# Bonus sums moved behind the prep and tied to gate blocks; keys and betas relaid so that one 128x128 transpose serves a head pair

## The chip, the core and the metric

The kernel runs on one core of a Trainium2 chip, in one launch. The metric is the device time in microseconds (us) of that launch. The engines are named as in the profile: PE is TensorE (PEld its weight load), DVE is VectorE, ACT is ScalarE, POOL is GpSimd, SP is SyncE. ACT, SP and POOL also issue DMAs; an engine's queue of issues stands in line with its instructions.

## What is computed

The reference is one block of a hybrid encoder on a sequence of 512 frames of width 1024: an input projection, an RWKV-7 branch (8 heads of 64) beside a gated linear recurrence, a merge by gates, cross-attention on 256 memory rows, and a gated feed-forward part. The change is all in the RWKV-7 branch. Cut to what matters of it:

```python
kk = k * k_k                       # then made of unit length for each head
k  = k * (1.0 + (a - 1.0) * k_a)   # the keys; the betas are kk * a
S_t = S_{t-1} diag(w_t) + (S_{t-1} a_t) b_t^T + v_t k_t^T
y_t = S_t r_t                      # a_t = -kk, b_t = kk * a
y   = group_norm(y) * lnx_g + lnx_b
bonus = jnp.sum(r * k * r_k, axis=-1, keepdims=True) * v
out = (y + bonus) * g
```

The bonus is a sum over the 64 channels of each head of r·k·r_k, times v. It doesn't enter the recurrence; it is added after the group norm.

## The kernel before

Channels lie on the 128 partitions (two heads of 64, a *pair*), the 512 frames run along the free axis. There are 4 pairs (NPAIR) and 8 chunks of 64 frames (NC). A float32 product is made as three fp32r matmuls of a high and a low part (mm3, L160 to L162), so a projection block of 128 output channels (`in_ps`) takes 24 matmuls of 512 columns, and its weights come by SP's queue as `win_r`, are split on ACT (`win_h`, L114) and on DVE (`win_l`, L115).

The input projection runs 14 RWKV blocks first (IN_RWKV) and then the 24 blocks of IN_REST, of which 16 are gate blocks: projection, sigmoid on ACT (`gs`), and a store to the DRAM buffer dG from ACT's queue. Blocks 22 to 24 (NEARLY = 3) are written ahead of the last pair's prep, the others after. They are the filler that keeps PE at work beside the RWKV steps.

For each pair j come, in this order: prep (L543 on: low-rank products, decay, unit length of kk), prep2 (which multiplies keys and betas by the inverse decay into KBt, L576 to L580, and writes AK), scores (16 products of 128 columns each per half, PE L605, masked by DVE into BZ and AK, L609 and L610; BZ goes out to dM), and bonus. The bonus multiplies r, k and r_k on DVE (`pr`, L586), splits the product into `bo_h` (ACT, L154) and `bo_l` (DVE, L155), sums over each head by two matmuls against a block of ones (`bo`, L156 and L157), multiplies by v (DVE, L589), adds lnx_b (ACT, L590) and stores to dBo[j] in DRAM from ACT's queue (L591).

After the four pairs, the prep's pool (pp) is closed and its memory is used again. `Zt` (the inverse of 32x32 triangles, solved on DVE, L655 to L661) takes over memory of it: its first memset, on DVE, waits until the store of the last pair's `pr` to dBo has landed. `Nm` is read back from dM for the solve. Then 32x32 products (zh, L687, and zo, L695), and the recurrence over 8 chunks: per chunk the products vr, x, y, u and s, and `rows_kb` (L741 to L748), which turns keys and betas of the next chunk from columns into rows by 8 transposes on PE (L746), each of 64 partitions by 128 columns, four into each of two PSUM banks ("kv" and "s"), and two copies on ACT (L747) into KBr. The group norm (L815 on) loads the bonus back from dBo (L821).

The order of the work on each engine is set by a scheduler from the order of the program text, priorities and dependences; each engine then runs its own list in order, so that an instruction that waits holds all that stands behind it on its engine.

Of the kernel before, what the change touches and what calls it, by code (L numbers as in the profile page):

```python
# [9 lines left out]
F32 = mybir.dt.float32  # L10
# [7 lines left out]
P = 128  # L18
# [12 lines left out]
IN_RWKV = [12, 13, 4, 5, 0, 1, 8, 9, 6, 7, 2, 3, 10, 11]  # L31
IN_REST = [22, 23, 24, 25, 26, 27, 28, 29, 30, 31, 32, 33, 34, 35, 36, 37, 14, 15, 16, 17, 18, 19, 20, 21]
NEARLY = 3
IN_ORDER = IN_RWKV + IN_REST


# [17 lines left out]
def hybrid_block_kernel(ctx: ExitStack, tc: tile.TileContext, xT_d, mT_d, pv_d, cst_d, win_d, wk_d, wv_d,  # L54
# [118 lines left out]
    def dense(ps, units, rhs, nkb, nsum=0):  # L173

        for kb in range(nkb):
            wh, wl = units.next()
            rh, rl = rhs(kb)
            ins = mm3(ps, wh, wl, rh, rl, kb == 0, kb == nkb - 1)
            if kb * nsum % nkb < nsum:
                sum_behind(ins)  # L180

    class Split:

# [294 lines left out]
    pa_ctx = ExitStack()  # L478
    pa = pa_ctx.enter_context(tc.tile_pool(name="pa", bufs=1, reuse_waits="tile"))
    BZ = pa.tile([P, NPAIR * NC, P], F32, tag="AR", name="BZ")  # L480
    KBt = big.tile([P, NPAIR, 2 * NC + 1, HD], F32, tag="x16", name="KBt")
    vT = pa.tile([P, NPAIR, T], F32, name="vT")
    AK = pa.tile([P, 2, NPAIR * NC, P], F32, tag="SC", name="AK")
    PC = pa.tile([P, NPAIR, NC], F32, name="PC")
# [22 lines left out]
    for i in range(2):  # L507
        with tc.issue_after(wdma[-1].ins):
            nc.sync.dma_start(lraw[i], lup_d[i])
    uin = Units(win_d, "win")  # L510


    NSUM = {12: 1, 13: 1, 4: 1, 5: 1, 0: 1, 1: 1, 8: 1, 9: 1, 6: 2, 7: 2, 2: 2, 3: 2, 10: 2, 11: 2,
            22: 2, 23: 1, 27: 1, 28: 1, 29: 1, 15: 4, 16: 4, 17: 4, 18: 4, 19: 4, 20: 3, 21: 2}

    def inproj(i):
        ps = mm_ps(f"in_ps{i}")
        dense(ps, uin, lambda kb: (h2[:, 0, kb, :], h2[:, 1, kb, :]), KB, NSUM.get(i, 0))
        return ps

    def evac_shift(ps, blk, out):
# [39 lines left out]
    def prep2(j, pk, pr, at, Pi, Pp):  # L561
        c3 = lambda a: a.rearrange("p (c t) -> p c t", t=HD)
        kk = pp.tile([P, T], F32, tag="kk", name=f"kk{j}")
        S.activation(kk, pk, AF.Copy, scale=par("k_k", j))
        sq = pp.tile([P, T], F32, tag="q", name=f"sq{j}", bufs=2)
        S.activation(sq, kk, AF.Square)
        ps = rw_ps(f"ss{j}")
        sum_exact(ps, bonesr, sq, tp, "xb", f"ss{j}")
        tab.rsqrt(sq, ps, 1.0, eps[:, 2:3])
        V.scalar_tensor_tensor(kk, sq, 1e12, kk, ALU.min, ALU.mult)  # L570
        jc = slice(j * NC, (j + 1) * NC)
        for e in range(2):
            hs = half[e]
            V.scalar_tensor_tensor(AK[hs, e, jc, 0:HD], c3(kk)[hs], -1.0, Pp[hs, :, 0:HD], ALU.mult, ALU.mult)
        V.tensor_tensor(kk, kk, at, ALU.mult)
        V.tensor_tensor(KBt[:, j, 1::2, :], c3(kk), c3(Pi), ALU.mult)  # L576
        S.activation(at, at, AF.Identity, scale=par("k_a", j), bias=oka[:, j:j + 1])
        V.tensor_tensor(pk, pk, at, ALU.mult)
        V.tensor_tensor(KBt[0:HD, j, 2::2, :], c3(pk)[0:HD], c3(Pi)[0:HD], ALU.mult)
        V.tensor_tensor(KBt[HD:P, j, 0:2 * NC:2, :], c3(pk)[HD:P], c3(Pi)[HD:P], ALU.mult)  # L580
        for e in range(2):
            hs = half[e]
            V.tensor_tensor(AK[hs, e, jc, HD:P], c3(pr)[hs], Pp[hs, :, 1:], ALU.mult)

    def bonus(j, pk, pr):
        V.scalar_tensor_tensor(pr, pr, par("r_k", j), pk, ALU.mult, ALU.mult)  # L586
        ps = rw_ps(f"bo{j}")
        sum_exact(ps, bonesr, pr, tp, "xb", f"bo{j}")
        V.tensor_tensor(pr, ps, vT[:, j, :], ALU.mult)  # L589
        S.activation(pr, pr, AF.Identity, bias=par("lnx_b", j))  # L590
        nc.scalar.dma_start(dBo[j], pr)  # L591

    def kb_cols(j, e, c):
        return KBt[half[e], j, 2 * c + 1 - e:2 * c + 3 - e, :].rearrange("p a t -> p (a t)")

    def scores(j):
        for e in range(2):
            hs, oh = half[e], half[1 - e]  # L600
            for cg in range(2):
                ps = rw_ps(f"sc{j}_{e}_{cg}")
                i0 = j * NC + cg * 4
                for i in range(4):
                    PE.matmul(ps[:, i * P:(i + 1) * P], kb_cols(j, e, cg * 4 + i), AK[hs, e, i0 + i, :],  # L605
                              start=True, stop=True)
                p3 = ps.rearrange("p (c t) -> p c t", t=P)
                m3 = scmask.unsqueeze(1).to_broadcast([P, 4, P])
# [12 lines left out]
    for jp in range(2):  # L621
# [10 lines left out]
        for j in js:  # L632
            if j == 3:
                for i in IN_REST[:NEARLY]:
                    gate_block(i - 22)
            at, L, Pp = prep(j)
            prep2(j, pks[j], prs[j], at, L, Pp)
            scores(j)
            bonus(j, pks[j], prs[j])

    pp_ctx.close()
    pq_ctx = ExitStack()
    pq = pq_ctx.enter_context(tc.tile_pool(name="pq", bufs=1, reuse_waits="tile"))
    YB = pq.tile([P, 4, T], F32, name="YB")


    with tc.tile_pool(name="pz", bufs=1, reuse_waits="tile") as pz:
# [91 lines left out]
        return UV  # L739

    def rows_kb(c):  # L741
        KBr = ch.tile([P, 2, NPAIR, HD], F32, tag="KBr", name=f"KBr{c}", bufs=2)
        for e in range(2):
            ps = ch_ps(f"kbr{c}_{e}", ("kv", "s")[e])
            for j in range(NPAIR):
                PE.transpose(ps[:, j * HD:(j + 1) * HD], kb_cols(j, e, c), ident[half[e], half[e]])  # L746
            S.copy(KBr[:, e], j3(ps[:, 0:256]))  # L747
        return KBr  # L748

    def pc_b(c):  # L750
# [2 lines left out]
    def chunk(c, UV, KBr, SP):  # L753
# [22 lines left out]
        if not last:  # L776
            nUV = rows_v(c + 1)
            pss = ch_ps(f"s{c}", "s")
            for j in range(NPAIR):
                for e in range(2):  # L780
                    PE.matmul(pss[half[e], j * HD:(j + 1) * HD], KBr[:, e, j, :], UV[:, e, j, :],
                              start=True, stop=True)
        for j in range(NPAIR):
            for e in range(2):
# [633 lines left out]
```

## Time and profile before

| | |
|---|---|
| time, 3 runs | 913.08, 912.09, 909.4 us; median 912.09 |
| the profiled execution | 909.73 us, its span 908.0 us |
| PE busy | 890.5 us (98% of the span) |
| DVE, ACT, POOL busy | 687.4, 510.4, 129.3 us |
| chain that ended last | PE 28%, DVE 1%, the rest below 1% |

The profile is of one execution. It gives the busy time of each engine, the waits of each engine with what ended them, and every instruction with its start and length. A matmul's length overlaps the next one's, so that PE's price for a matmul is read from one start to the next. An idle time in brackets behind a row is that of the engine just before the instruction, with what ended it.

### The profile page before, as it was taken

The numbers are of one execution on the slowest core, as the hardware profiler recorded it, in microseconds if no ns is written. First come the engines' busy times: TensorE is split into PE (matmuls) and PEld (weight loads), VectorE is DVE, ScalarE is ACT, GpSimd is POOL, SyncE is SP. The second block draws the span as 40 slices with busy tenths as digits, with TensorE's granted clock in tenths as the row PEclk, the third lists the DMA queues.
The fourth block names the chain that finished last, engine by engine and source line by source line (L and its number), as shares of the span: only waits on it lengthen the run. The fifth ranks groups of instructions, "written<-read, shape, count | busy, mean of one in ns | idle before, by whom it ended". The sixth has DMA issues, their size and how long they took to land. (4 is left out here: it accounts for less than half of the span.)

```text
span 908.0 us, 15914 instructions
## 1 busy us (share of the span) xinstructions
PE 890.5 (98%) x6218; PEld 776.1 (85%) x6218; DVE 687.4 (76%) x1096; ACT 510.4 (56%) x779; POOL 129.3 (14%) x159
## 2 busy tenths in 40 slices
PE   7999999999999999999999999999999999999996
PEld 6988877788877777887887778999999999999996
DVE  7884598776957585776565568788998888999674
ACT  6674675542236675234454446765665556767663
POOL 0102222010011212001112211111111111201100
PEclk9999999999999999999999999999999999999999
DMA  8878899667499749858788868898989998998963
GB/s 276 277 263 230 186 237 208 179 165 206 139 205 246 167 106 194 258 180 223 210 243 190 177 152 185 240 273 247 280 249 290 258 316 251 248 277 222 269 197 93
DMA packets 102411, 200.07 MB, mean 220 GB/s; under 512 B 25344, under 2 KB 36736, under 8 KB 102272
## 3 DMA queue, kind: packets, MB, share of 16 engines
q1 hardware_dynamic: 69504, 119.75, 41.0%
q0 software_dynamic: 25504, 67.38, 36.8%
q10 hardware_dynamic: 7328, 11.92, 3.9%
q8 instruction: 49, 0.80, 0.3%
q14 instruction: 26, 0.21, 0.1%
HBM read 187.75 MB, written 77.59 MB: 292 GB/s over the span
## 5 line engine op out<-in xcount | busy, mean ns | idle before, releaser
L126 ACT CAST wfi_h<-wfi_r 128x1024 fp32r<-128x1024 f32 x77 | 81.0, 1052 | 76.8 <-PE fx_ps L161 21.1
L160 PE MATMUL in_ps<-hT,win_h 128*128 128x512 f32 x304 | 121.9, 402 | 0.8 <-DVE pr L525 0.7
L162 PE MATMUL in_ps<-hT,win_l 128*128 128x512 f32 x304 | 120.8, 398 | 0.0
L161 PE MATMUL in_ps<-hT,win_h 128*128 128x512 f32 x304 | 120.6, 398 | 0.0
L127 DVE TENSOR_TENSOR wfi_l<-wfi_r,wfi_h 128x1024 fp32r<-128x1024 f32 x77 | 94.0, 1221 | 23.5 <-ACT wfi_h L126 23.3
L425 POOL DMA_DIRECT2D dS<-in_wfi x66 | 66.5, 1044 | 267.0 <-PE in_ps L160 132.4
L114 ACT CAST win_h<-win_r 128x1024 fp32r<-128x1024 f32 x38 | 39.8, 1048 | 71.9 <-PE in_ps L161 70.9
L115 DVE TENSOR_TENSOR win_l<-win_r,win_h 128x1024 fp32r<-128x1024 f32 x38 | 46.4, 1221 | 32.6 <-ACT win_h L114 32.5
L160 PEld LDWEIGHTS in_ps<-hT,win_h 128*128 128x128 f32 x304 | 57.0, 187 | 15.6 <-DVE pr L525 1.1
L161 PEld LDWEIGHTS in_ps<-hT,win_h 128*128 128x128 f32 x304 | 57.0, 188 | 14.0 <-issue 0.7
L162 PEld LDWEIGHTS in_ps<-hT,win_l 128*128 128x128 f32 x304 | 57.0, 187 | 13.9 <-issue 0.2
L461 POOL DMA_DIRECT2D dOs<-in_wfo x54 | 39.9, 804 | 186.0 <-PE fx_ps L160 50.9
L1245 DVE TENSOR_TENSOR wfo_l<-wfo_r,wfo_h 128x1024 fp32r<-128x1024 f32 (+1 forms) x39 | 47.2, 1210 | 13.6 <-ACT wfo_h L1244 13.5
L1244 ACT CAST wfo_h<-wfo_r 128x1024 fp32r<-128x1024 f32 (+1 forms) x39 | 40.4, 1038 | 28.2 <-PE oyz_ps L161 9.8
L161 PE MATMUL fx_ps<-hr,wfi_h 128*128 128x256 f32 x176 | 49.7, 282 | 0.0
L162 PE MATMUL fx_ps<-hr,wfi_l 128*128 128x256 f32 x176 | 49.7, 282 | 0.0
L160 PE MATMUL ox_ps<-go,wfo_h 128*128 128x256 f32 x176 | 49.6, 282 | 0.1
L160 PE MATMUL fyz_ps<-hq,wfi_h 128*128 128x256 f32 x176 | 49.3, 280 | 0.4 <-ACT p L1173 0.4
L160 PE MATMUL fx_ps<-hq,wfi_h 128*128 128x256 f32 x176 | 49.5, 281 | 0.0
L160 PE MATMUL fx_ps<-hr,wfi_h 128*128 128x256 f32 x176 | 49.4, 281 | 0.0
L162 PE MATMUL ox_ps<-go,wfo_l 128*128 128x256 f32 x176 | 49.3, 280 | 0.0
L161 PE MATMUL ox_ps<-go,wfo_h 128*128 128x256 f32 x176 | 49.3, 280 | 0.0
(418 smaller groups left out, 2727.8 us busy)
## 6 DMA issues: line engine op xcount, KB each, us to landing
dS<-in_wfi POOLq DMA_DIRECT2D x66, 512.0 KB, 8.4
wfi_r<-dS SPq DMA_DIRECT2D x44, 512.0 KB, 6.9
win_r<-in_win SPq DMA_DIRECT2D x38, 512.0 KB, 5.0
wfi_r<-in_wfi SPq DMA_DIRECT2D x33, 512.0 KB, 5.6
dS<-dS POOLq DMA_DIRECT2D x22, 512.0 KB, 5.7
dOs<-in_wfo POOLq DMA_DIRECT2D x12, 512.0 KB, 7.8
wv_r<-in_wv SPq DMA_DIRECT2D x8, 512.0 KB, 4.9
dG<-gs ACTq DMA_DIRECT2D x16, 256.0 KB, 2.6
```

The costliest lines, as they stand in the source:

```text
L114: S.copy(hi[:, o:o + n], raw[:, o:o + n])
L115: V.tensor_tensor(lo[:, o:o + n], raw[:, o:o + n], hi[:, o:o + n].bitcast(F32), ALU.subtract)
L126: S.copy(hi, raw)
L127: V.tensor_tensor(lo, raw, hi.bitcast(F32), ALU.subtract)
L160: first = PE.matmul(ps, lh, rh, start=start, stop=False, **kw)
L161: PE.matmul(ps, lh, rl, start=False, stop=False, **kw)
L162: PE.matmul(ps, ll, rh, start=False, stop=stop, **kw)
L425: return lambda: nc.gpsimd.dma_start(s(out), src, **kw)
L461: yield lambda k=k, w=w, src=src: nc.gpsimd.dma_start(dO[n, m][:, k * P:(k + w) * P], src, **kw)
L1244: S.copy(hi[:, :n], raw[:, :n])
L1245: V.tensor_tensor(lo[:, :n], raw[:, :n], hi[:, :n].bitcast(F32), ALU.subtract)
```

## The change

There are two parts.

*The bonus.* Inside the loop over pairs, only the product is left (`bonus_terms`): `pr` is stored to dBo[j] as it is. After the prep's pool is closed, the four products are loaded again (`bt`, ACT's queue), rounded by ACT into `bhi`, and the rest is taken by DVE into `blo`. Then gate blocks 25 to 29 (up to NMID = 8) follow, and after each from the second on the two sum matmuls of a pair, held by `issue_after` until the first product of the last mm3 of that gate block has issued. The product with v, lnx_b and the store to dBo[j] go with them (`bs`). `bhi` takes the memory that YB has later; `bt` and `bs` share two buffers.

*The layout.* KBt loses its one spare column group. In one partition half the keys stand before the betas, in the other the betas before the keys, so that the columns of one chunk are a full 128x128 square for both heads. `rows_kb` becomes 4 transposes of 128x128 into one bank and one ACT copy of 128x512, and the writes of KBt become four DVE operations on 64 partitions for each pair, where there were one on 128 and two on 64.

```diff
+NMID = 8
@@ dense
+        return ins
@@
-    KBt = big.tile([P, NPAIR, 2 * NC + 1, HD], F32, tag="x16", name="KBt")
+    KBt = big.tile([P, NPAIR, 2 * NC, HD], F32, tag="x16", name="KBt")
@@ inproj
-        dense(ps, uin, lambda kb: (h2[:, 0, kb, :], h2[:, 1, kb, :]), KB, NSUM.get(i, 0))
+        last_in = dense(ps, uin, lambda kb: (h2[:, 0, kb, :], h2[:, 1, kb, :]), KB, NSUM.get(i, 0))
@@ prep2
-        V.tensor_tensor(KBt[:, j, 1::2, :], c3(kk), c3(Pi), ALU.mult)
-        V.tensor_tensor(KBt[0:HD, j, 2::2, :], c3(pk)[0:HD], c3(Pi)[0:HD], ALU.mult)
-        V.tensor_tensor(KBt[HD:P, j, 0:2 * NC:2, :], c3(pk)[HD:P], c3(Pi)[HD:P], ALU.mult)
+        for e in range(2):
+            hs = half[e]
+            V.tensor_tensor(KBt[hs, j, e::2, :], c3(kk)[hs], c3(Pi)[hs], ALU.mult)
+            V.tensor_tensor(KBt[hs, j, 1 - e::2, :], c3(pk)[hs], c3(Pi)[hs], ALU.mult)
@@ bonus
+    def bonus_terms(j, pk, pr):
         V.scalar_tensor_tensor(pr, pr, par("r_k", j), pk, ALU.mult, ALU.mult)
+        nc.scalar.dma_start(dBo[j], pr)
+    def bonus(j, hi, lo, after):
         ps = rw_ps(f"bo{j}")
-        sum_exact(ps, bonesr, pr, tp, "xb", f"bo{j}")
-        V.tensor_tensor(pr, ps, vT[:, j, :], ALU.mult)
-        S.activation(pr, pr, AF.Identity, bias=par("lnx_b", j))
-        nc.scalar.dma_start(dBo[j], pr)
-    def kb_cols(j, e, c):
-        return KBt[half[e], j, 2 * c + 1 - e:2 * c + 3 - e, :].rearrange("p a t -> p (a t)")
+        with tc.issue_after(after.ins):
+            PE.matmul(ps, bonesr, hi, start=True, stop=False)
+            PE.matmul(ps, bonesr, lo, start=False, stop=True)
+        bt = tp.tile([P, T], F32, tag="xb", name=f"bs{j}", bufs=2)
+        V.tensor_tensor(bt, ps, vT[:, j, :], ALU.mult)
+        S.activation(bt, bt, AF.Identity, bias=par("lnx_b", j))
+        nc.scalar.dma_start(dBo[j], bt)
+    def kb_cols(j, hs, c):
+        return KBt[hs, j, 2 * c:2 * c + 2, :].rearrange("p a t -> p (a t)")
@@ the pairs, and after them
-            bonus(j, pks[j], prs[j])
+            bonus_terms(j, pks[j], prs[j])
-    YB = pq.tile([P, 4, T], F32, name="YB")
+    bhi = pq.tile([P, NPAIR, T], F32R, tag="YB", name="bhi")
+    blo = [tp.tile([P, T], F32R, tag=("ga", "gx")[j % 2], name=f"blo{j}", bufs=2) for j in range(NPAIR)]
+    for j in range(NPAIR):
+        bt = tp.tile([P, T], F32, tag="xb", name=f"bt{j}", bufs=2)
+        nc.scalar.dma_start(bt, dBo[j])
+        S.copy(bhi[:, j, :], bt)
+        V.tensor_tensor(blo[j], bt, bhi[:, j, :].bitcast(F32), ALU.subtract)
+    for k, i in enumerate(IN_REST[NEARLY:NMID]):
+        gate_block(i - 22)
+        if k:
+            bonus(k - 1, bhi[:, k - 1, :], blo[k - 1], last_in)
+    YB = pq.tile([P, 4, T], F32, tag="YB", name="YB")
@@ rows_kb
-        for e in range(2):
-            ps = ch_ps(f"kbr{c}_{e}", ("kv", "s")[e])
-            for j in range(NPAIR):
-                PE.transpose(ps[:, j * HD:(j + 1) * HD], kb_cols(j, e, c), ident[half[e], half[e]])
-            S.copy(KBr[:, e], j3(ps[:, 0:256]))
+        ps = ch_ps(f"kbr{c}", "kv")
+        for j in range(NPAIR):
+            PE.transpose(ps[:, j * P:(j + 1) * P], kb_cols(j, slice(0, P), c), ident)
+        S.copy(KBr, ps.rearrange("p (j i) -> p j i", i=P))
@@ the later blocks
-    for i in IN_REST[NEARLY:]:
+    for i in IN_REST[NMID:]:
```

How the lists of the engines change where the prep ends. On DVE, before, the steps from the last masked scores to the first of the solve; `pr` is the last pair's product, `bo_l` its low part, the second `pr` the product with v:

```order
L610 TENSOR_TENSOR AK<-sc_1_1_1718,cst 64x512
L586 SCALAR_TENSOR_TENSOR pr_1354<-pr_1354,pv,pk_1278 128x512
L717 SCALAR_TENSOR_TENSOR cst<-cst 128x128
L115 TENSOR_TENSOR win_l_2809<-win_r_2806,win_h_2808 128x1024
L155 TENSOR_TENSOR bo_l<-pr_1354,bo_h 128x512
L589 TENSOR_TENSOR pr_1354<-bo_1727,vT 128x512
L115 TENSOR_TENSOR win_l_2843<-win_r_2840,win_h_2842 128x1024
L655 MEMSET Zt 128x1024
L656 MEMSET Zt 128x32
L115 TENSOR_TENSOR win_l_2877<-win_r_2874,win_h_2876 128x1024
L660 TENSOR_TENSOR zz<-Zt,Nm 128x1
```

The same stretch of DVE now, from the split of weights behind the last `pr` on; `blo_1710` to `blo_1713` are the low parts of pairs 0 to 3, `bs` the products with v:

```order
L116 TENSOR_TENSOR win_l_2778<-win_r_2775,win_h_2777 128x1024
L681 MEMSET Zt 128x1024
L665 TENSOR_TENSOR blo_1710<-bt_1714,bhi 128x512
L665 TENSOR_TENSOR blo_1711<-bt_1718,bhi 128x512
L682 MEMSET Zt 128x32
L116 TENSOR_TENSOR win_l_2812<-win_r_2809,win_h_2811 128x1024
L665 TENSOR_TENSOR blo_1712<-bt_1722,bhi 128x512
L602 TENSOR_TENSOR bs_1802<-bo_1799,vT 128x512
L665 TENSOR_TENSOR blo_1713<-bt_1726,bhi 128x512
L602 TENSOR_TENSOR bs_1844<-bo_1841,vT 128x512
L686 TENSOR_TENSOR zz<-Zt,Nm 128x1
```

The memset of Zt stands ahead of the low parts of all four pairs, and the solve's first step behind them and behind two products with v.

On PE now, 34 projection matmuls after the last pair's scores; `bo_1799` and `bo_1841` are the sums of pairs 0 and 1, each a matmul of the high part (L599) and one of the low part (L600):

```order
L599 MATMUL bo_1799<-bhi,bonesr 128x512
L161 MATMUL in_ps_1848<-hT_0_89,win_h_1851 128x512
L599 MATMUL bo_1841<-bhi,bonesr 128x512
L162 MATMUL in_ps_1848<-hT_1_90,win_h_1851 128x512
L163 MATMUL in_ps_1848<-hT_0_89,win_l_1852 128x512
L600 MATMUL bo_1799<-blo_1710,bonesr 128x512
L161 MATMUL in_ps_1890<-hT_0_89,win_h_1893 128x512
L162 MATMUL in_ps_1890<-hT_1_90,win_h_1893 128x512
L600 MATMUL bo_1841<-blo_1711,bonesr 128x512
```

Before, PE had in this stretch the two matmuls of the last pair only, five projection matmuls apart; those of the other pairs lay in the prep.

On ACT now, from the rounding of pairs 0 and 1 on; `bt_1722` and `bt_1726` are the loads of pairs 2 and 3:

```order
L664 CAST bhi<-bt_1714 128x512
L664 CAST bhi<-bt_1718 128x512
L663 DMA bt_1722<-dBo 128x512
L115 CAST win_h_2811<-win_r_2809 128x1024
L663 DMA bt_1726<-dBo 128x512
L664 CAST bhi<-bt_1722 128x512
```

The load of pair 2 takes the buffer of pair 0's `bt`, so it stands behind the step on DVE that reads that buffer last.

## Rows read from the trace of the kernel before

**Rows 1.** PE's waits: line waited for, total us, times, longest.

```profile
PE bo L157 <- DVE bo_l L155: 0.6, 2, 0.4
PE bo L156 <- DVE AK L610: 0.5, 1, 0.5
```

**Rows 2.** Busy us by stretch: PE, PEld, DVE, ACT, POOL; clock, DMA share, GB/s.

```profile
175.00:265.00 90.00, 90.00 (x399) 71.66 (x399) 68.12 (x109) 33.23 (x42) 5.31 (x6) 1.00 0.64 177
```

**Rows 3.** Timeline of PE, first chunk's transposes: start, us, line, operation.

```profile
285.85 0.46 PE L746 MATMUL kbr<-cst,KBt 64*128 64x64 f32 x4
286.24 0.50 PE L162 MATMUL in_ps<-hT,win_l 128*128 128x512 f32 x1
286.57 0.39 PE L160 MATMUL in_ps<-hT,win_h 128*128 128x512 f32 x1
286.80 0.40 PE L161 MATMUL in_ps<-hT,win_h 128*128 128x512 f32 x1
```

**Rows 4.** Timeline of PE, 128x128 float32 transposes of the attention.

```profile
476.31 0.41 PE L1028 MATMUL prT_ps<-cst,ex 128*128 128x128 f32 x2
476.48 0.48 PE L162 MATMUL q_ps<-hx,wq_l 128*128 128x512 f32 x1
```

**Rows 5.** Instructions on the tile KBt: duration in ns, minimum, median, maximum.

```profile
L576 DVE TENSOR_TENSOR KBt<-kk,L x4: 683/686/693, 113.2 to 185.1; 128x512 f32<-128x512 f32 x4
```

**Rows 6.** Timeline of PE after the last pair's scores.

```profile
191.36 0.50 PE L160 MATMUL in_ps<-hT,win_h 128*128 128x512 f32 x1
...
198.29 0.39 PE L160 MATMUL in_ps<-hT,win_h 128*128 128x512 f32 x1
...
199.92 0.39 PE L161 MATMUL in_ps<-hT,win_h 128*128 128x512 f32 x1
```

**Rows 7.** Timeline of DVE from the last bonus product to the solve.

```profile
194.80 0.73 DVE L586 SCALAR_TENSOR_TENSOR pr<-pr,pv,pk 128x512 f32<-128x512 f32 x1
...
197.16 0.69 DVE L155 TENSOR_TENSOR bo_l<-pr,bo_h 128x512 fp32r<-128x512 f32 x1
...
206.98 0.91 DVE L655 MEMSET Zt<- 128x1024 f32 x1 [3.62 <-DMA dBo<-pr]
...
212.45 0.16 DVE L660 TENSOR_TENSOR zz<-Zt,Nm 128x1 f32<-128x1 f32 x1 [3.22 <-DMA Nm<-dM]
```

**Rows 8.** Timeline of ACT and its queue in the same stretch.

```profile
195.89 0.61 ACT L154 CAST bo_h<-pr 128x512 fp32r<-128x512 f32 x1
...
197.11 0.33 ACTq L619 DMA_DIRECT2D dG<-gs  x1
```

**Rows 9.** DMA queues from 197.5 to 201.5: packets, MB, share of 16 engines.

```profile
q0 software_dynamic: 214, 0.44, 101.5%
```

**Rows 10.** DMA issues from 195 to 210: count, KB each, median us to landing.

```profile
dG<-gs ACTq DMA_DIRECT2D x3, 256.0 KB, 7.0
```

**Rows 11.** DMA issues from 208 to 210.

```profile
dG<-gs ACTq DMA_DIRECT2D x1, 256.0 KB, 4.6
```

**Rows 12.** DMA issues from 172 to 174.

```profile
dBo<-pr ACTq DMA_DIRECT2D x1, 256.0 KB, 2.0
```

**Rows 13.** Busy us by stretch at the end (PE first; clock third from last).

```profile
900.40:903.50 3.10, 0.05 (x1) 0.00 (x0) 2.35 (x4) 1.29 (x5) 0.00 (x0) 1.00 0.22 63
903.50:908.00 4.50, 0.00 (x0) 0.00 (x0) 0.15 (x1) 0.00 (x0) 0.00 (x0) 0.50 0.67 189
```

**Rows 14.** Timeline of PE at the start: 256-column matmuls before and after 16.0.

```profile
6.20 0.58 PE L160 MATMUL k_ps<-m,wk_h 128*128 128x256 f32 x1 [6.20 <-ACT m L286]
...
15.59 0.41 PE L160 MATMUL k_ps<-m,wk_h 128*128 128x256 f32 x1
15.81 0.40 PE L161 MATMUL k_ps<-m,wk_h 128*128 128x256 f32 x1
...
16.75 0.28 PE L162 MATMUL k_ps<-m,wk_l 128*128 128x256 f32 x1
16.87 0.28 PE L160 MATMUL k_ps<-m,wk_h 128*128 128x256 f32 x1
```

More of the change, by code (lines that the diff above doesn't have):

```diff
@@ L510, in hybrid_block_kernel @@
     uin = Units(win_d, "win")
+    last_in = None
     NSUM = {12: 1, 13: 1, 4: 1, 5: 1, 0: 1, 1: 1, 8: 1, 9: 1, 6: 2, 7: 2, 2: 2, 3: 2, 10: 2, 11: 2,
@@ L516, in inproj @@
     def inproj(i):
+        nonlocal last_in
         ps = mm_ps(f"in_ps{i}")
-        dense(ps, uin, lambda kb: (h2[:, 0, kb, :], h2[:, 1, kb, :]), KB, NSUM.get(i, 0))
+        last_in = dense(ps, uin, lambda kb: (h2[:, 0, kb, :], h2[:, 1, kb, :]), KB, NSUM.get(i, 0))
         return ps
@@ L583, in prep2 @@
             V.tensor_tensor(AK[hs, e, jc, HD:P], c3(pr)[hs], Pp[hs, :, 1:], ALU.mult)
-    def bonus(j, pk, pr):
+    def bonus_terms(j, pk, pr):
         V.scalar_tensor_tensor(pr, pr, par("r_k", j), pk, ALU.mult, ALU.mult)
+        nc.scalar.dma_start(dBo[j], pr)
+    def bonus(j, hi, lo, after):
         ps = rw_ps(f"bo{j}")
-        sum_exact(ps, bonesr, pr, tp, "xb", f"bo{j}")
-        V.tensor_tensor(pr, ps, vT[:, j, :], ALU.mult)
-        S.activation(pr, pr, AF.Identity, bias=par("lnx_b", j))
-        nc.scalar.dma_start(dBo[j], pr)
-    def kb_cols(j, e, c):
-        return KBt[half[e], j, 2 * c + 1 - e:2 * c + 3 - e, :].rearrange("p a t -> p (a t)")
+        with tc.issue_after(after.ins):
[7 more added lines that the diff above has]
+        return KBt[hs, j, 2 * c:2 * c + 2, :].rearrange("p a t -> p (a t)")
     def scores(j):
@@ L604, in scores @@
                 for i in range(4):
-                    PE.matmul(ps[:, i * P:(i + 1) * P], kb_cols(j, e, cg * 4 + i), AK[hs, e, i0 + i, :],
+                    PE.matmul(ps[:, i * P:(i + 1) * P], kb_cols(j, hs, cg * 4 + i), AK[hs, e, i0 + i, :],
                               start=True, stop=True)
@@ L741, in rows_kb @@
     def rows_kb(c):
-        KBr = ch.tile([P, 2, NPAIR, HD], F32, tag="KBr", name=f"KBr{c}", bufs=2)
-        for e in range(2):
-            ps = ch_ps(f"kbr{c}_{e}", ("kv", "s")[e])
-            for j in range(NPAIR):
-                PE.transpose(ps[:, j * HD:(j + 1) * HD], kb_cols(j, e, c), ident[half[e], half[e]])
-            S.copy(KBr[:, e], j3(ps[:, 0:256]))
+        KBr = ch.tile([P, NPAIR, P], F32, tag="KBr", name=f"KBr{c}", bufs=2)
+        ps = ch_ps(f"kbr{c}", "kv")
+        for j in range(NPAIR):
+            PE.transpose(ps[:, j * P:(j + 1) * P], kb_cols(j, slice(0, P), c), ident)
+        S.copy(KBr, ps.rearrange("p (j i) -> p j i", i=P))
         return KBr
@@ L780, in chunk @@
                 for e in range(2):
-                    PE.matmul(pss[half[e], j * HD:(j + 1) * HD], KBr[:, e, j, :], UV[:, e, j, :],
+                    PE.matmul(pss[half[e], j * HD:(j + 1) * HD], KBr[:, j, half[e]], UV[:, e, j, :],
                               start=True, stop=True)
```

## The prediction

> **What bounds the kernel now.** I read the waits of PE first, then the busy time by stretch, then the timelines of the places that the diff touches. PE is at work for 98% of the span, and between the prep and the recurrence it has no gap at all: 90.00 of 90.00 us from 175 to 265, in which DVE is busy for 68 and ACT for 33 [rows 2]. So inside the kernel a microsecond is won only by less work on PE or by one of its few waits, and every new wait of PE is paid in full, because its list runs in order and no other engine's slack can give it back. Two waits of PE belong to the bonus: 0.5 us before the first high part and 0.6 us in two waits for the low part [rows 1]. That is little, so I asked next what the new order makes PE wait for.
>
> 0.5% of this kernel is 4.6 us, about what a measurement can tell from no change.
>
> **The change part by part.**
>
> *The bonus leaves the prep.* The eight sum matmuls stay eight. The waits of 0.5 and 0.6 us go with them: 1.1 us [rows 1]. DVE gives up the low part, 0.69 us for each pair [rows 7], and gets one KBt operation more, which at 0.69 us costs as much; the two 64-partition halves of an operation cost as much each as the whole did, since the length goes with the 512 columns [rows 5]. The rest of the DVE work of the bonus (the product with v) leaves the prep too, so DVE is no later there. Bounds: 0 us, if PE then waits for the next DVE step of the same chain instead, to 2.1 us, if as much again goes in the shorter holds that the waits don't list. I take 1.1 us, the listed ones.
>
> *The layout.* Four of the old transposes take 0.39 us from their start to the next matmul (285.85 to 286.24), and the first projection matmul after them takes 0.33 instead of the 0.23 of the next one [rows 3]: a change of tile shape costs some 0.10 us. Taking 0.10 off the 0.39 leaves 0.07 for each, 4.6 us for all 64. The kernel before has no 128x128 transposes of KBt; the nearest row is the attention's, where two take 0.17 us up to the next matmul, which is 0.085 each [rows 4]. For 32 of them that is 2.7 us; if each takes as long as two old ones (0.14), 4.5. In the two orders of PE I count 16 changes of shape fewer, worth 1.6 us. So the gain is between 4.6 + 1.6 - 4.5 = 1.7 and 4.6 + 1.6 - 2.7 = 3.5 us; I take 2.5. The two ACT copies that become one lie beside this and cost nothing, with ACT at 33 of 90 us.
>
> Sum of what the change takes away: 1.1 + 2.5 = 3.6 us, all on PE.
>
> *The new wait.* The sums come 34 projection matmuls after the last scores. The first projection matmul after these scores starts at 191.36, and one takes 0.233 us (seven starts from 198.29 to 199.92) [rows 6]. With 0.10 for the shape, PE reaches the low part of pair 0, 39 matmuls on, at 191.36 + 0.10 + 9.1 = 200.55, in the clock of the profile before. It needs `blo` of pair 0, which on DVE's list stands behind the memset of Zt. That memset waits for the landing of the last `pr` store: before, it sat idle for 3.62 us until 206.98 for this very store [rows 7]. Before, only the solve stood behind it. Now the whole of PE does.
>
> The store itself comes earlier. The product ends at 195.53 [rows 7], and ACT's cast, 0.36 us later [rows 8], shows that ACT was then near its turn; I put the issue at 196.2. What it takes to land is the question that decides. In a quiet stretch such a store took 2.0 us [rows 12]; the three dG stores of the same size from the same queue between 195 and 210 took 7.0 in the median [rows 10], and one of them was issued at 197.11 [rows 8]. The reason stands in the queues: from 197.5 to 201.5 only POOL's software queue moved data, at 101% of the engines' time, and the hardware queues moved none [rows 9]. My store is issued 1.3 us before that burst and cannot have landed by its start, so I take it as held until the burst ends, like the dG store at 197.11, whose 7.0 would end at 204.1: landing at 204.0. Then memset 0.91 and low part 0.69 [rows 7], and 0.1 for the signals: 205.7. **PE waits 5.1 us.** The low part of pair 1 follows 0.69 later, as fast as PE needs it.
>
> The Trainium skill, page "DMA: Bandwidth & Descriptors", section "Queues, rings and completion order", says that an engine goes round the queues it has work for and changes at every packet. By that rule the store would pass between the software packets, and the sum would be that of the first rival below, -3.0 us instead of +2.2; the 4 us without a hardware packet [rows 9] speak against it here.
>
> Second, the load of pair 2 stands on ACT's list behind the low part of pair 0, since it takes its buffer. It is issued at 205.7 and lands 2.0 [rows 12] to 4.6 us later, as the dG store after 208 did [rows 11]; I take the middle, 3.3: 209.0, and with 0.61 of cast [rows 8] 209.6. PE would be there 14 matmuls after the low part of pair 0: 205.7 + 3.3 = 209.0. That is 0.6 to 0.7 us more; bounds 0 and, with a landing of 7.0 [rows 10], 4.3. Pair 3 is loaded close behind and finds PE 3 us further on, so it adds nothing. Together 5.8 us, bounds 0 and 9.4.
>
> *The solve.* Its first step on DVE now stands behind the low part of pair 3 and the product with v of pair 1. Pair 3's load is issued some 1 us after pair 2's, so these end near 212, where the solve began before for want of Nm, 212.45 [rows 7]. Two more products, 1.4 us, lie inside the solve. PE's products on it come up to 1.4 us later, but PE itself comes 5.8 us late, less what it saved; so this is hidden, unless the stall is absent.
>
> *Sum.* -3.6 + 5.8 = +2.2 us on the profiled execution's own 909.73: 911.9. That execution lies 2.4 us under the median of the three runs, so I put the change on the median: 912.1 + 2.2 = 914.3.
>
> **The rivals.**
>
> *The store isn't held* (chance 0.25). It lands 2.0 us after issue, at 198.2; memset and low part end at 199.8, before PE's 200.55. The load of pair 2 is issued then and is cast by 202.4 to 205.0 with landings of 2.0 and 4.6, where PE needs it at 203.8: 0 to 1.2 us. For: such stores have taken 2.0 us [rows 12], and by moving the issues the change can shift the software burst too. Against: rows 9 and 10. The time is 912.1 - 3.6 + 0.6 = 909.1, and up to 1 us more where the later solve shows. By the Trainium skill's rule on the queues this is what comes.
>
> *The stall costs PE its clock* (0.20). This one ends on the other side. At the end of the kernel the granted clock was 1.00 until 903.5 and 0.50 after, with no matmul begun after 900.4 but one short piece [rows 13]. At the start, after 6.2 us of idling, PE ran 256-column matmuls 0.22 us apart up to about 16, and 0.12 apart after [rows 14]: the 1.2 GHz level for some 10 us. A gap of 5.1 us inside the kernel is longer than the 3.1 at the end. If the clock falls in it, and PE needs as long as at the start to get it back, half of 10 us, 5 us, is lost; if half as long, 2.5. I take 4: 914.3 + 4 = 918.3. [...] Against: no row shows the clock falling between two stretches of dense work.
>
> *The gain is larger than listed* (0.07). Both upper bounds together, 2.1 + 3.5 = 5.6 us, and no stall: 906.5.
>
> **How the numbers follow.** The forecast, a store held and 5.8 us of stall at the full clock, has 0.48: 914.3. Slower by over 0.5%, above 916.7: 0.19 of the clock's case and 0.07 of the forecast's own (a stall above 8.2 us, when the second load lands late): 0.26. Faster by over 0.5%, below 907.5: the larger gain, 0.07, and 0.05 of the unheld store with the wider prep gain: 0.12. Within: 0.62. The range reaches down to the unheld store without any stall, 908.5, less 1 us for the spread of the runs (909.4 to 913.08), and up to the clock's case, 918.3, with 1.7 us for the same: 907.5 to 920.
>
> **What would show it.** Right: PE waits some 5 us at L600 for `blo`, DVE's Zt memset waits just before it for the dBo store, and a second, smaller wait stands at L599 for `bhi`. In the recurrence, transposes at L772 come 0.085 to 0.14 us apart, and the same stretch is 2 to 3 us shorter. The two bonus waits in the prep are gone. Wrong: PE has no wait over 1 us after the prep (then the store passed the burst); the granted clock shows a stretch at 0.50 after the stall (then the time is above 916); or PE waits for pr or KBt in the prep as long as it did for the bonus (then the 1.1 us are not there).

## The result, and the profile after

The changed kernel takes 914.66 us in the median of 22 runs, the kernel before 909.96 in the median of 22: a ratio of 1.0041, interval 1.0030 to 1.0052, so some 3.7 us slower. A run in the chip's slow state, here one of 1741.49 us, is left out of every ratio and every mean clock. The prediction was 914.3. The total came out as forecast; of its terms, the held store was not there, and a late load and the clock stood in its place.

The rows below are of one profiled execution of the changed kernel (916.91 us, its span 915.1; it is the longest of six runs, whose median is 914.09; the kernel before has 910.35 beside them). First PE's waits, the longest ones, as in [rows 1]:

```profile
PE k_ps L161 <- ACT m L288: 6.6, 1, 6.6
PE bo L599 <- ACT bhi L664: 4.7, 1, 4.7
PE in_ps L161 <- DVE pk L529: 1.1, 1, 1.1
```

The two bonus waits of [rows 1] are gone, and a wait of 4.7 us stands at the high part of a bonus sum. On PE's timeline it is the sum of pair 2, and the matmuls behind it are further apart than those ahead of it:

```profile
200.00 0.39 PE L600 MATMUL bo<-blo,bonesr 128*128 128x512 f32 x1
...
202.33 0.39 PE L163 MATMUL in_ps<-hT,win_l 128*128 128x512 f32 x1
207.45 0.79 PE L599 MATMUL bo<-bhi,bonesr 128*128 128x512 f32 x1 [4.73 <-ACT bhi L664]
208.04 0.63 PE L161 MATMUL in_ps<-hT,win_h 128*128 128x512 f32 x1
208.47 0.63 PE L162 MATMUL in_ps<-hT,win_h 128*128 128x512 f32 x1
...
211.12 0.39 PE L162 MATMUL in_ps<-hT,win_h 128*128 128x512 f32 x1
211.35 0.40 PE L163 MATMUL in_ps<-hT,win_l 128*128 128x512 f32 x1
```

The low parts of pairs 0 and 1 (the second of them at 200.00) have no wait. From 208.04 to 208.47 a matmul takes 0.43 us, from 211.12 on again 0.23. The busy time by stretch shows why; the clock is the third number from the end:

```profile
207.30:210.71 3.41, 3.26 (x8) 2.58 (x9) 2.77 (x4) 1.98 (x4) 0.00 (x0) 0.50 1.07 206
289.22:292.63 3.41, 3.41 (x22) 2.41 (x20) 0.77 (x2) 0.45 (x1) 0.27 (x1) 0.50 1.01 207
```

The granted clock is at 0.50, the 1.2 GHz level, for 3.41 us from the end of the wait on, and for another 3.41 us behind the 32x32 products of the solve, where PE has no wait ahead of it. The profiled execution of the kernel before has neither. PE is at work through nearly all of both, so each piece costs about half its length, 1.7 us.

On DVE, the rows that answer to [rows 7]:

```profile
193.57 0.73 DVE L592 SCALAR_TENSOR_TENSOR pr<-pr,pv,pk 128x512 f32<-128x512 f32 x1
...
196.71 0.91 DVE L681 MEMSET Zt<- 128x1024 f32 x1 [1.07 <-DMA dBo<-pr]
197.54 1.22 DVE L665 TENSOR_TENSOR blo<-bt,bhi 128x512 fp32r<-128x512 f32 x2
...
207.43 0.69 DVE L665 TENSOR_TENSOR blo<-bt,bhi 128x512 fp32r<-128x512 f32 x1 [5.84 <-ACT bhi L664]
```

and on ACT, to [rows 8]:

```profile
194.33 0.33 ACTq L593 DMA_DIRECT2D dBo<-pr  x1
...
198.20 0.33 ACTq L663 DMA_DIRECT2D bt<-dBo  x1
...
206.78 0.62 ACT L664 CAST bhi<-bt 128x512 fp32r<-128x512 f32 x1 [6.45 <-DMA bt<-dBo]
```

The last store of `pr` was issued at 194.33, 0.03 us after its product, and let the memset go at 196.71: it was not held. Its data went ahead of the software traffic. These are the DMA queues from 194.3 to 196.2 (q10 carries ACT's transfers; q0, the software queue, has its first packet at 196.22):

```profile
q10 hardware_dynamic: 144, 0.26, 36.7%
q1 hardware_dynamic: 481, 0.12, 36.6%
...
dBo<-pr ACTq DMA_DIRECT2D x1, 256.0 KB, 2.0
```

The load of pair 2 was issued at 198.20, behind the low part of pair 0 as the lists say, and its cast waited for it until 206.78: 8.6 us. That load is PE's 4.7 us.

Where the time went, by stretches of PE. Each number is the length of a stretch, from one landmark's first matmul to the next one's, less 0.2335 us for each 512-column matmul in it, so that filler which moved from one stretch to another doesn't count (one profiled execution each):

| stretch | before | changed | layout alone | bonus alone | all three repairs |
|---|---|---|---|---|---|
| first scores of pair 0 to those of pair 3 | 14.4 | 13.7 | 18.4 | 12.8 | 12.8 |
| those of pair 3 to the first product on the solve | 4.7 | 11.0 | 4.7 | 8.0 | 4.8 |
| from there to the first matmul of the y output (yb_ps) | 56.1 | 56.0 | 53.4 | 57.5 | 52.1 |
| from there to the last matmul | 350.2 | 351.4 | 350.9 | 349.7 | 350.6 |

The changed kernel loses 6.3 us in the second stretch and wins 0.7 in the prep. The third holds the recurrence: the layout alone shortens it by 2.7 us, and the changed kernel would be 1.8 us shorter there than before if the second piece of low clock, 1.7 us, didn't lie in it. The same stretch is 1.4 us longer in the bonus alone, with no wait and no low clock in it, so a reading of it to a few tenths says little. The last stretch is 1.2 us longer in the changed kernel; a wait of 0.7 us for DVE's `wfo_l` is a part of that, the rest is open.

### The profile page after: what moved, and what is told of

It reads as the page before. It is cut to its first block, busy times and chain, and to the rows that moved or that the text cites. A ratio compares the mean times of both kernels' runs of the same rounds, so it can differ in the third digit from the quotient of the medians.

```text
span 1739.7 us, 15879 instructions
## 1 busy us (share of the span) xinstructions
PE 1725.5 (99%) x6186; PEld 1377.5 (79%) x6186; DVE 703.3 (40%) x1100; ACT 515.6 (30%) x771; POOL 129.2 (7%) x159
## 4 chain that ended last, share of the span: by engine, by line
PE 99%; DMA 0%; DVE 0%; SPq 0%; ACT 0%; DVEq 0%; issue 0%
PE in_ps L161 8%; PE in_ps L162 8%; PE in_ps L163 8%; PE fx_ps L161 5%; PE fx_ps L163 5%; PE fx_ps L162 5%; PE fyz_ps L163 4%; PE fyz_ps L162 4%; PE fyz_ps L161 4%; PE ox_ps L162 2%; PE ox_ps L161 2%; PE ox_ps L163 2%; PE oyz_ps L163 2%; PE oyz_ps L161 2%; PE oyz_ps L162 2%; PE q_ps L162 2%
## 5 line engine op out<-in xcount | busy, mean ns | idle before, releaser
L163 PE MATMUL in_ps<-hT,win_l 128*128 128x512 f32 x304 | 206.5, 680 | 0.0
L162 PE MATMUL in_ps<-hT,win_h 128*128 128x512 f32 x304 | 206.0, 680 | 0.0
L161 PE MATMUL in_ps<-hT,win_h 128*128 128x512 f32 x304 | 205.4, 677 | 0.0
L162 PEld LDWEIGHTS in_ps<-hT,win_h 128*128 128x128 f32 x304 | 91.2, 300 | 49.1 <-issue 45.1
L161 PEld LDWEIGHTS in_ps<-hT,win_h 128*128 128x128 f32 x304 | 89.8, 295 | 50.5 <-issue 46.4
L163 PEld LDWEIGHTS in_ps<-hT,win_l 128*128 128x128 f32 x304 | 90.7, 298 | 49.3 <-issue 45.4
L161 PE MATMUL ox_ps<-go,wfo_h 128*128 128x256 f32 x176 | 77.7, 442 | 0.0
L163 PE MATMUL fyz_ps<-hq,wfi_l 128*128 128x256 f32 x176 | 77.6, 441 | 0.0
L161 PE MATMUL fx_ps<-hr,wfi_h 128*128 128x256 f32 x176 | 77.6, 441 | 0.0
L162 PE MATMUL fx_ps<-hr,wfi_h 128*128 128x256 f32 x176 | 77.5, 441 | 0.0
L162 PE MATMUL ox_ps<-go,wfo_h 128*128 128x256 f32 x176 | 77.4, 440 | 0.0
L161 PE MATMUL fx_ps<-hq,wfi_h 128*128 128x256 f32 x176 | 77.4, 440 | 0.0
L162 PE MATMUL fyz_ps<-hq,wfi_h 128*128 128x256 f32 x176 | 77.3, 439 | 0.0
L163 PE MATMUL ox_ps<-go,wfo_l 128*128 128x256 f32 x176 | 77.3, 439 | 0.0
L161 PE MATMUL fyz_ps<-hq,wfi_h 128*128 128x256 f32 x176 | 77.0, 437 | 0.0
L162 PE MATMUL fx_ps<-hq,wfi_h 128*128 128x256 f32 x176 | 76.9, 437 | 0.0
```

Of the source, the lines that this page charges most:

```text
L161: first = PE.matmul(ps, lh, rh, start=start, stop=False, **kw)
L162: PE.matmul(ps, lh, rl, start=False, stop=False, **kw)
L163: PE.matmul(ps, ll, rh, start=False, stop=stop, **kw)
```

## The experiments

The theories at the start: the *held store* (the forecast: DVE's memset waits for the last store, PE for the low part of pair 0, at full clock), the *lost clock*, and the *store not held*. The trace of the changed kernel itself brought a fourth: the *held load*.

**e0_after: the changed kernel as it is.** No edit.

> The changed kernel as it is, for a profile that can be compared. Held store: PE waits about 5 us at the low part of the bonus sums (L600) for blo, behind the Zt memset that waits for the last dBo store, and 0 to 4 us at the next high part (L599); 914 us against 910, with the granted clock at 1.00 throughout between 16 and 900. Lost clock: the same wait, but a stretch of several us at 0.50 behind it, worth 2 to 4 us of the loss. Store not held: no wait of PE over 1 us after the prep, and the loss lies elsewhere.

Measured: 914.09 us against 910.35, ratio 1.0040 (1.0023 to 1.0057). The wait of about 5 us is there, but not at the low part and not behind the memset; the clock falls. So the held store falls, and the lost clock is half right. Over 27 runs of the changed kernel the mean granted clock of the runs is 0.9946, over 79 of the kernel before 0.9973. Lost time is the length times the share that the clock lacks: 0.0027 x 914 = 2.5 us.

**e1_layout: the new layout in the kernel before.** The edit is the change's second part, cut here to two of its places:

```diff
+        for e in range(2):
+            hs = half[e]
+            V.tensor_tensor(KBt[hs, j, e::2, :], c3(kk)[hs], c3(Pi)[hs], ALU.mult)
+            V.tensor_tensor(KBt[hs, j, 1 - e::2, :], c3(pk)[hs], c3(Pi)[hs], ALU.mult)
@@ rows_kb
+            PE.transpose(ps[:, j * P:(j + 1) * P], kb_cols(j, slice(0, P), c), ident)
```

> The kernel before with the layout of keys and betas alone; the bonus stays in the prep. Held store and lost clock alike: 2.5 us faster than before (1.7 to 3.5), all in the recurrence. If the layout is worth nothing, or costs something by the extra DVE step in the prep, the loss of the changed kernel has another source than the sums: 0 to +1 us.

Measured: 911.64 us, ratio 1.0011 (0.9995 to 1.0027): no gain. The recurrence did get shorter. Here are its stretches (first `vr` to last `y`) by busy time, first the kernel before, then this one; both hold 51 matmuls of 512 columns:

```profile
284.96:342.57 57.61, 57.61 (x875) 42.79 (x875) 42.44 (x85) 38.49 (x77) 9.34 (x10) 1.00 0.69 147
```

```profile
289.22:343.34 54.12, 52.98 (x839) 39.91 (x839) 40.44 (x81) 35.00 (x66) 9.92 (x11) 1.00 0.76 159
```

3.5 us shorter, of which the stretch behind gives back 0.8. But the prep took 4 us more. Its waits, and the clock behind the second of them, which ends at 129.37; behind the first, at 147.87, it stays at 1.00:

```profile
PE bo L156 <- ACT bo_h L154: 1.9, 1, 1.9
PE in_ps L160 <- DVE pk L525: 1.8, 1, 1.8
```

```profile
129.80:133.10 3.30, 3.30 (x10) 2.53 (x9) 3.05 (x7) 2.90 (x4) 0.72 (x1) 0.50 0.70 191
```

With the bonus still in the prep, PE waits for DVE there, directly or by way of ACT's `bo_h`. The edit changes two things on DVE: it adds a KBt operation (0.69 us for each pair, [rows 5]) and puts the betas' products behind the step that scales the keys. Which of them makes PE wait isn't told apart by this run.

**e2_bonus: the bonus behind the prep, with the old layout.**

> The changed kernel with the old layout: the bonus behind the prep alone. Held store: the stall of 5.8 us less 1.1 us of waits in the prep, 4.7 us slower than before (about 2.5 us slower than the changed kernel). Lost clock: 6 to 9 us slower, with a stretch at 0.50. Store not held: within 1 us of before.

Measured: 913.53 us, ratio 1.0031 (1.0019 to 1.0043), 2.8 us slower. PE's longest wait between the start and the end of the kernel is at the same instruction, and 3.41 us of low clock follow it in the profiled execution:

```profile
PE bo L598 <- ACT bhi L663: 2.3, 1, 2.3
```

So most of the loss belongs to the bonus part: alone the layout is 1.0 us slower (an interval that holds no change) and the bonus 2.8, together 3.7, although the layout saves its 2.7 us in the recurrence. That the numbers nearly add up is no proof that the parts do: the wait is 2.3 us here and 4.7 in the changed kernel, and the mean granted clock over this kernel's runs is 0.9968, against 0.9972 of the kernel before beside them, so that the clock accounts for some 0.4 us of the 2.8 on the average.

**e3_poolset: the memsets of Zt on POOL.**

```diff
-        V.memset(Zt, 0.0)
+        nc.gpsimd.memset(Zt, 0.0)
```

> The changed kernel with the two memsets of Zt on POOL instead of DVE, so that the low parts on DVE no longer stand behind the landing of the last dBo store. Held store: the wait for the low part of pair 0 goes; what is left is the load of pair 2 or 3, 0 to 2 us; 2 to 3 us faster than before, 5 us faster than the changed kernel. Lost clock: the clock stays at 1.00 as well, so it gains as much again as the clock took, and the time is the same 907 to 908. If the wait of PE isn't the memset's, nothing changes against the changed kernel.

Measured: 914.96 us, ratio 1.0043 (1.0027 to 1.0060): the same as the changed kernel. This run, too, speaks against the held store. The load of pair 2 now leaves at once, and still waits:

```profile
194.75 0.33 ACTq L663 DMA_DIRECT2D bt<-dBo  x1
...
202.91 0.62 ACT L664 CAST bhi<-bt 128x512 fp32r<-128x512 f32 x1 [4.23 <-DMA bt<-dBo]
```

8.1 us from issue to landing, 3.2 us of PE's time at the high part. Counted from the first scores of pair 3, it was issued 1.6 us sooner than in the changed kernel and took as long: something holds the transfer itself.

**e4_later: the sums two gate blocks later.**

```diff
-NMID = 8
+NMID = 10
-        if k:
-            bonus(k - 1, bhi[:, k - 1, :], blo[k - 1], last_in)
+        if k > 2:
+            bonus(k - 3, bhi[:, k - 3, :], blo[k - 3], last_in)
```

> The changed kernel with the sums tied two gate blocks later (up to NMID = 10, the first sum behind the third of these blocks and so on). The load of pair 2 lands as late as in the changed kernel, but PE comes to its high part some 8 us later. Held load: no wait of PE for bhi or blo, no loss of the clock there; 2 to 3 us faster than before, 907 to 909. If the loss lies in the solve or in the products with v on DVE, which come later too, the time stays at 912 to 915.

Measured: 912.86 us, ratio 1.0027 (1.0012 to 1.0041). PE waits for neither `bhi` nor `blo`, and most of the loss stays. The place of the wait has moved:

```profile
PE zh L713 <- DMA ZA<-dZt: 2.9, 1, 2.9
```

The solve shares DVE with the low parts and the products with v. Counted from the first scores of pair 3, its first step comes at 25.8 us, when `Nm` has landed (25.3 in the changed kernel, 24.7 before), and the first half of its result, `ZA`, is back at 81.1 (79.7 in the changed kernel, 77.8 before). PE is there earlier now, and waits; and the clock is low for 6.83 us from there. A stall that is taken from one place is partly paid at the next one that was hidden behind it.

**e5_quiet and e8_quiet2: two of POOL's weight sums moved away.** The transfers behind gate blocks 28 and 29 go behind 32 and 33:

```diff
-            22: 2, 23: 1, 27: 1, 28: 1, 29: 1, 15: 4, ...
+            22: 2, 23: 1, 27: 1, 32: 1, 33: 1, 15: 4, ...
```

> The changed kernel with two of POOL's weight-sum transfers (those behind gate blocks 28 and 29) moved to blocks 32 and 33, so that the software queue is quiet while the load of pair 2 is out. Held by the software queue: the load lands 2 to 5 us after its issue instead of 8.6, PE's wait for bhi falls from 4.7 to 0 to 1 us, and the time to 908 to 910. If the load is held by the hardware queues' own traffic (the many small packets of Nm, the weights), the wait stays at 3 to 5 us and the time at 914.

> The kernel with the two weight-sum transfers moved (as in the run on the quiet queue) once more, in more rounds. Held by the software queue: 1.0 to 2.0 us faster than before, no wait for bhi. If the earlier run was luck: no difference from before.

Measured: 909.39 us, ratio 0.9984 (0.9964 to 1.0004), and again 909.65, 0.9989 (0.9975 to 1.0003). Both intervals just hold 1, so it isn't shown to be faster than before; against the changed kernel it wins some 5 us. The DMA queues from 199 to 206 in the changed kernel (packets, MB, share of the 16 engines), with the load of pair 3:

```profile
q1 hardware_dynamic: 1904, 0.75, 46.3%
q0 software_dynamic: 196, 0.37, 36.3%
q10 hardware_dynamic: 319, 0.56, 30.5%
...
Nm<-dM SPq DMA_DIRECT2D x1, 256.0 KB, 14.9
bt<-dBo ACTq DMA_DIRECT2D x1, 256.0 KB, 8.2
```

and from 197 to 206 in the quiet kernel:

```profile
q1 hardware_dynamic: 4115, 1.03, 59.0%
q10 hardware_dynamic: 572, 1.04, 44.6%
...
Nm<-dM SPq DMA_DIRECT2D x1, 256.0 KB, 7.3
bt<-dBo ACTq DMA_DIRECT2D x1, 256.0 KB, 5.2
```

The software queue (q0) is gone, the load takes 5.2 us instead of 8.2, that of pair 2, 3.9 instead of 8.6 (196.55 to its cast at 200.49), and PE's wait for `bhi` is gone in the first of these runs and 0.7 us in the second. So it was the software traffic that held the load, not the small packets of Nm, which went on. It had held Nm as well: Nm now lands after 7.3 us instead of 14.9, and the solve's first step comes 20.1 us after the first scores of pair 3 instead of 25.3. This edit therefore takes away two delays, that of the load and that of the solve. The clock is no clean account here: in the first of the two profiled executions it is low for 6.83 us behind the 32x32 products, without a wait ahead, in the second not at all before the end.

**e6_early: pair 2's load ahead of the last scores, into a buffer of its own.** The edit is cut; further down, the rounding of pair 2 reads `bt2`.

```diff
+            if j == 3:
+                bt2 = tp.tile([P, T], F32, tag="gx", name="bt2", bufs=2)
+                nc.scalar.dma_start(bt2, dBo[2])
             scores(j)
```

> The changed kernel with the load of pair 2 into a buffer of its own (one of the later gx tiles), issued ahead of the last pair's scores, some 20 us before the software traffic. Only pair 3's load is still out then. Held load: PE's wait for pair 2 goes, and one of 1 to 3 us comes at pair 3, 14 matmuls further on; 910 to 912. If it is the place on ACT's list and not the transfer that is late, the wait at pair 2 goes and none follows: 908.

Measured: 909.84 us, ratio 0.9992 (0.9976 to 1.0009). The wait goes, and pair 3 brings 0.2 us, not 1 to 3: its load, the only one left, lands nearly in time, after 6.9 us. But as in the run with later sums, the solve comes up, and 3.41 us of low clock behind it:

```profile
PE zh L719 <- DMA ZA<-dZt: 1.8, 1, 1.8
```

**e7_fill: PE kept at work in the gap.**

```diff
+            for _ in range(20 if j == 2 else 0):
+                PE.matmul(ps, bonesr, bhi[:, 1, :], start=True, stop=True)
@@ the gate blocks; last_in is now a list, one for each mm3 of the block
-        if k:
-            bonus(k - 1, bhi[:, k - 1, :], blo[k - 1], last_in)
+        if k in (1, 2):
+            bonus(k - 1, bhi[:, k - 1, :], blo[k - 1], last_in[7])
+        if k == 4:
+            bonus(2, bhi[:, 2, :], blo[2], last_in[3])
+            bonus(3, bhi[:, 3, :], blo[3], last_in[7])
```

> The changed kernel with 20 more matmuls of 512 columns (4.7 us of PE work whose sums are overwritten) just ahead of pair 2's high part, which is tied to the last gate block. PE is as late for what follows as in the changed kernel, but works where it stood still. If a part of the loss is the clock that falls in PE's wait: the mean granted clock goes back from 0.9945 to 0.997 and the time falls by 1.5 to 2.5 us, to 912. If the loss is the wait alone: 914 as in the changed kernel.

Measured: 924.48 us, ratio 1.0149. The clock never fell in the profiled execution (0.997 in the mean, the low part only at the end), and in the stretch of the former wait PE worked on without a gap. That is what the lost clock expects of this execution; over the four runs the mean is 0.9958 (0.993 to 0.998), so in some of the others it did fall. And the time went up by 10 us where it should have gone down: the scheduler changed the order far behind the edit as well. The projection blocks that fill PE beside the group norm are used up sooner, the norm's sums (gv) stand among the matmuls of the y output, and PE waits there as in no other run, for instance:

```profile
PE gv L159 <- DVE gv_l L157: 2.1, 2, 1.2
PE mix_ps L162 <- ACT mg L967: 1.9, 1, 1.9
```

As a measurement of what the clock costs it is spoilt, and the split of the loss into wait and clock is not shown by an experiment; it rests on the rows of the changed kernel and on the granted clocks of the runs.

**e9_kkfirst: the quiet kernel, with the betas ahead of the keys on DVE.**

```diff
+        for e in range(2):
+            hs = half[e]
+            V.tensor_tensor(KBt[hs, j, e::2, :], c3(kk)[hs], c3(Pi)[hs], ALU.mult)
         S.activation(at, at, AF.Identity, scale=par("k_a", j), bias=oka[:, j:j + 1])
         V.tensor_tensor(pk, pk, at, ALU.mult)
```

> The same with the two products of the betas ahead of the step on ACT that scales the keys, where the kernel before had its one product. If the wait of 1.1 us for pk, which the new layout leaves in the prep, comes from the betas standing behind the keys on DVE: it goes, 1 us faster than the quiet run, 908. If the prep waits for DVE's work as a whole: the same as the quiet run.

Measured: 909.46 us, ratio 0.9991 (0.9977 to 1.0004), as the quiet run. In the prep the wait of 1.1 us for pk did go and the stretch is 0.9 us shorter (12.8 against 13.7); but the order moved the sums closer to the scores (pair 2's high part stands 35 matmuls of 512 columns behind them instead of 53), and the wait for pair 2's load came back, with 3.41 us of low clock behind it:

```profile
PE bo L601 <- ACT bhi L666: 1.8, 1, 1.8
```

**e10_all: quiet queue, early load and betas first together.**

> Three repairs on the changed kernel at once: the two weight-sum transfers moved, the load of pair 2 into a buffer of its own ahead of the last scores, the betas ahead of the keys on DVE. If the load's wait, the clock that it costs and the betas' place are what keeps the change from its gain of some 3.5 us: 907 (0.996 to 0.998 of before), no wait for bhi and none for pk. If each repair only moves a wait on: 909 to 910, as the quiet run.

Measured: 905.65 us, ratio 0.9949 (0.9937 to 0.9962): 4.6 us faster than before, and by the two ratios (0.9949 and 1.0040) some 8 us faster than the changed kernel. From the last pair's scores to past the recurrence PE has next to no gap (0.05 us) and no lost clock:

```profile
189.00:266.00 77.00, 77.00 (x360) 61.01 (x360) 60.96 (x100) 26.99 (x35) 4.90 (x5) 1.00 0.76 199
266.00:345.00 79.00, 78.95 (x1159) 60.05 (x1156) 55.27 (x105) 54.06 (x92) 16.80 (x18) 1.00 0.78 170
```

That is the gain that the forecast put on the change without its new wait, and 1 us more. It isn't shown to be the change's alone: the moved weight sums are no part of it, and the kernel before was not run with them. In that kernel PE has no gap from 175 to 265 [rows 2] that they could close; what an earlier solve is worth there wasn't tried. Of the repairs, the quiet queue and the early load were run alone on the changed kernel, the betas first only on top of the quiet queue; none of these is shown to beat the kernel before, the three together are. Whether two would do stays open.

**e11_layout2: the layout alone, betas first.**

> The kernel before with the layout alone, as in the first run on it, and the betas ahead of the keys on DVE. If that run lost its gain in the prep because DVE wrote the betas late: PE's waits of 1.8 us for pk and 1.9 for bo_h go, the clock stays in the prep, and it is 2 to 3 us faster than before, 907.5. If DVE's additional operation itself costs the gain: the same as that run, 0 to 1 us slower than before.

Measured: 917.76 us, ratio 1.0081 (1.0069 to 1.0094): both answers missed. With the bonus in the prep, this order lets PE run into a wait for DVE, and the clock is at 0.50 for 13.65 us:

```profile
PE in_ps L160 <- DVE pr L525: 5.5, 1, 5.5
```

```profile
137.10:150.80 13.70, 12.39 (x45) 10.48 (x46) 12.49 (x21) 2.84 (x4) 1.16 (x1) 0.50 0.42 74
```

The same order of the betas that takes 0.9 us off the prep without the bonus in it costs 6 us with it. What it is in the order of DVE that leaves `pr` so late was not taken apart further.

## Why the prediction was right, and where only its sum was

*The bound.* Right: a new wait of PE is paid in full. In the changed kernel the wait of 4.7 us and the 1.7 us of clock behind it are, to 0.1 us, the 6.3 us that the second stretch lost.

*The bonus leaves the prep: 1.1 us.* 0.7 in the changed kernel. The two waits of [rows 1] are gone, and another of 1.1 us for pk stands there now, the lower bound's case in part. With the old layout the prep wins 1.6 us, and with the new one and the betas first as much (12.8 both times). So the KBt operation more costs PE nothing, as forecast; what was wrong is that "DVE is no later there": the betas behind the keys cost 0.9 us of PE's time (13.7 against 12.8).

*The layout: 2.5 us.* Right as far as one execution each can tell: 2.7 in the run with it alone, 2.5 in e11_layout2 (53.6 against 56.1). Summed over the trace up to what follows each group, the 64 old transposes take 6.5 us and the 32 new ones of the layout alone 4.3. The price of one lies between the bounds ahead of a projection matmul: four take 0.41 us, 0.10 each, here on the timeline of the kernel with all repairs:

```profile
292.93 0.66 PE L780 MATMUL kbr<-cst,KBt 128*128 128x128 f32 x4
293.34 0.48 PE L163 MATMUL in_ps<-hT,win_l 128*128 128x512 f32 x1
```

Ahead of a small product a group of four takes up to 0.59.

*The held store: 5.1 us of PE's waiting for pair 0.* Wrong, and it is the step that failed. The forecast put the issue 0.7 us behind the product and 1.3 us ahead of the burst, so that the store "cannot have landed by its start". With the sums gone from ACT's list, the store left 0.03 us behind the product and 1.9 us ahead of the burst, and landed after 2.0 us, as the first rival had it; the memset waited 1.07 us and PE not at all. Inside the burst it might well have been held: in the kernel before, the last store of `pr`, issued at 199.97, took 6.7 us. That transfers of ACT's queue take longer beside software traffic was right, but it was the load of pair 2, issued at 198.20, that met it. Nor was the burst a wall here; the trace of the changed kernel from 196.5 to 199 shows both queues moving data:

```profile
q0 software_dynamic: 117, 0.24, 72.4%
q10 hardware_dynamic: 103, 0.21, 25.2%
```

where [rows 9] had software packets only. The Trainium skill's rule (page "DMA: Bandwidth & Descriptors", section "Queues, rings and completion order"), by which an engine goes round its queues packet by packet, agrees with these rows; it doesn't say why no hardware packet came through in the 4 us of [rows 9], and no run here shows that.

*The load of pair 2: 0.7 us, bounds 0 and 4.3.* The mechanism was right, the buffer of pair 0 and the place on ACT's list too; the size was off, since the forecast had the burst end before this load is issued. It landed after 8.6 us instead of 3.3, beyond the upper bound of 7.0, and cost 4.7 us. The two errors nearly cancel: 5.8 us forecast, 4.7 measured.

*The clock.* Given 0.20 as a rival at 4 us, and left out of the sum because no row showed it falling between two stretches of dense work. It fell, and cost 2.5 us in the mean over the runs. In the profiled execution it is 1.7 us for the piece behind the wait and 1.7 for the one before the recurrence; where it lies in the other runs isn't on record. The mistake in its price was to take the 10 us of the start [rows 14] as the measure: the pieces here are 3.41 us long.

*The solve.* Right: its steps on DVE take 42.7 us instead of 40.6 from the first to the last, which the stall hides in the changed kernel, and where the stall was taken away (later sums, early load) PE waited 2.9 and 1.8 us for it.

*The sum.* -0.7 for the prep, -2.7 for the layout, 4.7 for the wait and 2.5 for the clock give +3.8 us, against 3.7 measured by the ratio. The agreement is closer than the terms are: the wait is that of the longest of six executions, the layout's gain that of another kernel, and the 1.4 us by which the third stretch is longer in the bonus alone have no term. The forecast, +2.2, had a larger wait and no clock. That its 914.3 lies so near the measured 914.66 is luck in part: it stands on 912.09 us for the kernel before, the median of three runs, where 22 runs give 909.96. The time lies within 0.5% of before, the likeliest of the three outcomes. Of the signs named for being right, the long wait stood at L599 for `bhi`, not at L600 for `blo`; of those for being wrong, the clock at 0.50 came, at a time below the 916 us named with it. The gain of 3.6 us that the forecast put on the rest fits the 4.6 of the kernel with all three repairs, with the reservation made there.

## What to carry to other kernels

When PE is the bound and a step is moved into its stream as "filler", follow each operand back to its transfer and ask which traffic that transfer will meet; the price of a short wait can be the wait and the clock that falls behind it. A stall removed at one place may only uncover the next (here the solve), so a repair that shows no gain alone isn't refuted. And where two terms of opposite sign come out in a forecast's sum, only the profile shows whether it was right or lucky.

## What was not expected of the hardware

In eight of the profiled executions a wait of PE of 1.8 to 5.5 us in the middle of dense work came with a stretch at the 1.2 GHz level (matmuls of 512 columns 0.43 us apart instead of 0.23), which began inside the wait or at most 1.1 us behind it. It is 3.41 us long in six of them (the changed kernel, the layout alone, the bonus alone, the memsets on POOL, the early load, e9_kkfirst), 6.83 with the later sums and 13.65 in e11_layout2. Two waits of 1.9 us, in the layout alone and in e7_fill, came without one. Behind the 32x32 products of the solve the clock fell in two executions without a wait ahead, in the changed kernel and in the first of the quiet kernel.

The loads of pairs 2 and 3, 256 KB each, took 3.9 to 6.0 us in the two executions of the quiet kernel, beside hardware traffic alone, and 5.8 to 8.6 us in the kernels with the two software transfers of 512 KB near them (the changed kernel, the bonus alone, the memsets on POOL, the later sums, the early load).
